# Modulation vectors of a two-layer diffusion step: two k tiles per TensorE visit in layer 0, and layer 1's second-norm shift and scale on VectorE during layer 0's FFN

## The chip, the cores and the metric

One NeuronCore of a Trainium2 chip runs the whole program. The metric is device time in microseconds (us), of which less is better. TensorE (PE) multiplies matrices, VectorE (DVE) and ScalarE (ACT) work elementwise, GpSimd (POOL) helps, and SyncE (SP) issues nearly all loads. Each of these runs its own stream of instructions in the order in which the program wrote it.

## The reference, cut to what matters

Two layers work on 384 tokens of 1,024 channels (128 context tokens and 256 latent tokens). Each layer computes six modulation vectors from a conditioning vector, for the context (`c_ctx`) and for the latents (`c`):

```
mod = (silu(cvec) @ w_mod + b_mod)                 # cvec: 1024, w_mod: 1024 x 6144, per layer
sh1, sc1, g1, sh2, sc2, g2 = split(mod, 6)         # v = 0, 1, 2, 3, 4, 5 in the kernel
hn = rmsnorm(x, g_norm1) * (1 + sc1) + sh1
x = x + g1 * mixer(hn)                             # attention, gated linear attention, pooling, gates, w_out
hn = rmsnorm(x, g_norm2) * (1 + sc2) + sh2
x = x + g2 * ((silu(hn @ w_ff_gate) * (hn @ w_ff_up)) @ w_ff_down)
```

The change concerns only when, and on which engine, those vectors of `w_mod` are computed. One vector takes eight k tiles of `w_mod`, each 128 x 1024 numbers (512 KB).

## The kernel before, in words

**Weights.** A class `Kern` first plans a list of segments (`seg`) and then plays it (`run`, with `pump` between segments). Every big weight tile is a *unit*: SP loads it into one of `RAWB` = 4 buffers `raw` (512 KB, or 448 KB for a 7-tile piece of `w_ff_down`; line 1170 issues most of them), ACT copies it into a rounded high part `wh` (line 151), DVE subtracts to get the low part `wl` (line 155), and `mm3` (line 219) multiplies: `wh` by both parts of the activations and `wl` by the high part, so 24 matmuls of 384 columns for eight k tiles, 21 for seven. There are `HB` = 3 pairs of `wh` and `wl`, so the split runs two units ahead of PE. A `raw` buffer is free again when its `wl` is done. `pump` issues the load of a unit only when the unit four places earlier in the ring has been freed, and the buffer that a load gets is the one that the program released longest ago.

**Modulation tiles** use the same ring of `raw` buffers, but are not split. They come in two kinds:

- `mod_vec` (lines 462 to 477): four TensorE matmuls per k tile (line 472) take the tile straight from `raw`; the buffer is free when PE has read it. `filler` (line 516) puts one such k tile into the plan at each call: after each `rb` tile and after each gate tile of the mixer's branches, 24 places per layer. Layer 0 uses them for vectors 2, 4 and 3 (24 tiles), layer 1 for vectors 4 and 3 (16 tiles). One such k tile is called a *visit* below.
- `mod_vec_acc` (line 483): per k tile two DVE instructions add to the two sums `P` and `A` (line 496 for the first k tile, line 498 for the other seven). The buffer is free when the second has run. After the eighth tile `fin` waits five turns and then lets PE add over the partitions by eight `pick` matmuls (line 510, four on `P` and four on `A`, each with two records in the trace); `mod_fin` (line 520) copies the result (line 523), waits and transposes it (line 530). The next vector's `P` and `A` use the same memory, so its line 496 must wait for those picks.

`accq` is the queue of DVE tiles of an FFN; `acc_step` puts the next of them into the plan. Layer 0's FFN has 32 of them: vector 5 of layer 0 and vectors 1, 0 and 2 of layer 1. Layer 1's FFN has 8.

**FFN** (`plan_ffn`): 22 pairs of a gate and an up unit; after each pair j > 1 one `acc_step`. Then the down projection: 8 output tiles n, each of three pieces of 8, 7 and 7 k tiles, 24 pieces in all; after every second piece one `acc_step`, as long as there is something in `accq`:

```
if (n * 3 + k0 // 7) % 2:
    self.acc_step()
```

So in layer 0 there are 20 steps behind gate/up pairs and 12 in the down projection. After it the row stage loads the first 256 KB tiles of layer 1's mixer (line 1183).

Of the kernel before, what the change touches and what calls it, by code (L numbers as in the profile page):

```python
# [15 lines left out]
KT = D // 128  # L16
# [14 lines left out]
class Kern:  # L31
    def __init__(self, ctx, tc, a, o):
        self.tc, self.nc, self.a, self.o = tc, tc.nc, a, o
        pool = lambda n, b, **k: ctx.enter_context(tc.tile_pool(name=n, bufs=b, **k))
        self.sb = pool("sb", 1)
        self.ps = pool("ps", 1, space=bass.MemoryType.PSUM)
        self.units = []
        self.segs = []
        self.threads = []
        self.wt = {}  # L40
        self.raw = {}
        self.n_split = 0
        self.n_raw = 0
        self.n_held = 0
        self.freed = set()
        self.ringpos = []
        self.n_ring = 0
        self.split_lim = 0
        self.mid_used = {}
        self.fillq = []  # L50
        self.accq = []
        self.htmp = {}
        self.pool_sub = set()
        self.low = []
        self.pend = set()
        self.late = []
        self.mark = 0
        self.modT = {}
        self.modfin = {}
        self.vec = {}  # L60
        self.nctr = 0
        self.sa_i = 0
        self.held = []
# [420 lines left out]
    def mod_vec_acc(self, l, v):  # L484

        st = {}

        def step(kt):
            def fn(u):
                nc = self.nc  # L490
                if kt == 0:
                    st["acc"] = [self.t(n, [128, 1024]) for n in ("P", "A")]
                for c, acc in enumerate(st["acc"]):
                    s = self.sc[:, kt, c:c + 1]
                    if kt == 0:
                        nc.vector.tensor_scalar(acc, self.raw[u], s, None, op0=ALU.mult)
                    else:
                        nc.vector.scalar_tensor_tensor(out=acc, in0=self.raw[u], scalar=s, in1=acc,  # L498
                                                       op0=ALU.mult, op1=ALU.add)
                if kt == KT - 1:  # L500
                    self.modfin[l, v] = self.spawn(fin())
            return [self.mod_unit(l, v, kt)], fn, 0

        def fin():
            for _ in range(5):
                yield
            ps = self.psa()
            for c, acc in enumerate(st["acc"]):
                for j in range(4):
                    self.nc.tensor.matmul(ps[32 * j:32 * j + 32, 0:256], self.pick[:, 32 * c:32 * c + 32],  # L510
                                          acc[:, j * 256:j * 256 + 256], start=c == 0, stop=c == 1,
                                          tile_position=(0, 32 * j))
            yield from self.mod_fin(l, v, ps)
        return [lambda kt=kt: step(kt) for kt in range(KT)]

    def filler(self):
        if self.fillq:
            self.seg(*self.fillq.pop(0)(None))

    def mod_fin(self, l, v, ps):  # L520
        nc = self.nc
# [979 lines left out]
    def plan_ffn(self, l, final):  # L1501
# [3 lines left out]
        def act_g(pg):  # L1505
            tt = self.t("tt", [128, T], bufs=2)
            nc.scalar.activation(tt, pg, AF.Tanh, scale=0.5)  # L1507
            self.late.append(lambda: nc.vector.scalar_tensor_tensor(
                out=tt, in0=tt, scalar=1.0, in1=pg, op0=ALU.add, op1=ALU.mult))
            return tt  # L1510
# [13 lines left out]
        def first(u, i):  # L1524

            ps = st[i] = self.pd() if i else self.psa(hold=True)

            def after(k):
                if i == 0 and k == 4:
                    st["norm"] = self.norm()  # L1530
                    next(st["norm"])
                if i == 1 and k == 2:
                    st["rs"] = next(st["norm"])
                    self.run_low()
                if i == 1:
                    self.hn_after(k, 3, l, 32, 24, st.get("rs"), (4, 1))
                if i == 1 and k == 3:
                    st["bb"] = self.t("rsmall", [128, 2, 2])
                    st["rest"] = self.post(st["t"][0], st[0], st["rs"], st["bb"][:, 0])
                    self.held.clear()  # L1540
            if i == 1:
                st["t"] = self.t("kn", [128, T]), self.t("KA", [128, T])
            self.mm_side((ps[:, 0:T + 2],), (u,), self.xw, after, 0)
# [23 lines left out]
        for j in range(NF):  # L1567
            ug, uu = ucol("w_ff_gate", j), ucol("w_ff_up", j)
            if j == 0:
                self.seg([ug], lambda u: first(u, 0))  # L1570
                self.seg([uu], lambda u: first(u, 1))
            elif j == 1:
                self.seg([ug, uu], second)
            else:
                hold = {}

                def fg(u, hold=hold):
                    ps = self.pd()
                    self.mm3(ps[:, 0:T], u, KT, self.xs, 0, True, True)
                    hold[0] = act_g(ps[:, 0:T])  # L1580

                def fu(u, j=j, hold=hold):
                    ps = self.pd()
                    self.mm3(ps[:, 0:T], u, KT, self.xs, 0, True, True)
                    act_u(j, hold[0], ps[:, 0:T])
                self.seg([ug], fg)
                self.seg([uu], fu)
            if j > 1:
                self.acc_step()

        us = tuple((lambda k, z=z: st["u"][k // 4][z][:, k % 4, :]) for z in range(2))
        for n in range(KT):
            hold = {}
            if not final and n == 6:
                self.seg([], lambda: self.load_gl(l + 1), 0)
            for k0, nk in ((0, 8), (8, 7), (15, 7)):
                u = self.unit((l, "fd", n, k0), self.w_cols(a["w_ff_down"][l], n * 128, nk=nk, k0=k0), nk * 128)

                def fn(u, n=n, k0=k0, nk=nk, hold=hold):
                    if k0 == 0:  # L1600
                        self.flush()
                        hold[0] = self.pd()
                    ps = hold[0][:, 0:T]
                    self.mm3(ps, u, nk, us, k0, k0 == 0, k0 == 15)
                    if k0 == 15:
                        if n == 0:
                            self.join(self.modfin[l, 5])
                        self.residual(l, n, ps, 40)
                        if final:
                            g_ = self.spawn(self.out_tile(n))  # L1610
                            if n == KT - 1:
                                self.join(g_)
                        else:
                            self.ssq_add(n)
                            st.setdefault("pre", []).append(n)
                            if n == 5:
                                self.load_sqrt()
                    if not final and n >= 4 and st["pre"]:
                        if not st.get("joined"):
                            st["joined"] = True  # L1620
                            for v in range(2):
                                self.join(self.modfin[l + 1, v])
                        self.pre(l + 1, st["pre"].pop(0), 8, 0)
                self.seg([u], fn)
                if (n * 3 + k0 // 7) % 2:
                    self.acc_step()

    def acc_step(self):
# [19 lines left out]
@with_exitstack  # L1648
def tile_hybrid_dit_step(ctx: ExitStack, tc: tile.TileContext, a, o):
    k = Kern(ctx, tc, a, o)  # L1650
    k.RAWB, k.HB = 4, 3
    with tc.manual_schedule():
        for l in range(L):
            for v in (2, 4, 3) if l == 0 else (4, 3):
                k.fillq += k.mod_vec(l, v)
        for l in range(L):
            k.plan_layer(l)
            for ll, v in ((l, 5), (l + 1, 1), (l + 1, 0), (l + 1, 2)):
                if ll < L:
                    k.accq += k.mod_vec_acc(ll, v)  # L1660
            k.plan_ffn(l, l + 1 == L)
            assert not k.accq
        assert not k.fillq
        k.head()
        k.run()
# [66 lines left out]
```

## Time and profile before

| what | value |
|---|---|
| median of 3 runs | 1341.04 us (1338.82 to 1345.76) |
| the profiled execution's own time | 1340.77 us |
| its span on the core | 1338.6 us |
| mean granted clock of TensorE | 0.989 |
| DVE, ACT, POOL busy | 859.0 us (64%), 597.3 us (45%), 194.6 us (15%) |
| DMA queue of SP | 196.68 MB, 52.1% of 16 engines |

The span is the time between the first and the last instruction on the core; the run's own time has 2.2 us around it. A busy share is the time in which an engine works on instructions. For a wait, the trace gives the idle time and what ended it, in the form `[4.14 <-DMA raw]`.

### The profile page before, as it was taken

The page shows a single profiled execution, that of the slowest core. Times are in us where ns is not written, and L with a number is a line of the kernel's source. Part 1 is how long each engine was busy: PE and PEld are TensorE (multiplying, and loading weights), DVE is VectorE, ACT ScalarE, POOL GpSimd, SP SyncE. Part 2 cuts the span into 40 slices and gives each one's busy share as a digit, 9 for nine tenths or more (in the row PEclk, how much of TensorE's full clock was granted, in tenths as well). Part 3 has the DMA queues.
Part 4 walks back from the last instruction along what each step waited for, and adds up shares of the span by engine and source line. Part 5 has one row for each costly group of instructions (what it writes and reads, how often), then busy time and mean ns, then how long its engine had stood idle before and what let it go on. Part 6 is the DMA issues. An engine that isn't in the chain of part 4 may idle for free.

```text
span 1338.6 us, 23459 instructions
## 1 busy us (share of the span) xinstructions
PE 1297.1 (97%) x9285; PEld 1205.5 (90%) x9285; DVE 859.0 (64%) x1500; ACT 597.3 (45%) x1104; POOL 194.6 (15%) x232
## 2 busy tenths in 40 slices
PE   6998999999999999999999899999999999999998
PEld 4786788889998999999988777888999899999998
DVE  4497866354568768676877987754546777544432
ACT  5655365343356333332446644543435643333221
POOL 1177000010033000000123850001101300000000
PEclk9998999999999999999999999999999999999999
DMA  9942454656543656665745325456344366444442
GB/s 288 242 102 80 144 143 131 166 146 180 151 126 110 193 172 201 177 197 170 206 135 144 102 83 165 121 154 174 95 126 126 95 185 192 143 126 120 127 133 61
DMA packets 297788, 198.51 MB, mean 148 GB/s; under 512 B 24560, under 2 KB 282384, under 8 KB 297680
## 3 DMA queue, kind: packets, MB, share of 16 engines
q1 hardware_dynamic: 296928, 196.68, 52.1%
q8 instruction: 73, 1.20, 0.4%
q0 software_dynamic: 608, 0.28, 0.1%
q14 instruction: 35, 0.29, 0.1%
q10 hardware_dynamic: 144, 0.07, 0.0%
HBM read 194.64 MB, written 2.36 MB: 147 GB/s over the span
## 4 chain that ended last, share of the span: by engine, by line
PE 81%; DVE 7%; DMA 3%; issue 3%; ACT 3%; POOL 1%; SPq 1%; ACTq 0%; DVEq 0%; POOLq 0%
PE d L219 59%; PE d L1418 8%; PE d L1350 2%; DMA m<-in_w_mod_dram 2%; PE m L472 2%; DVE wl L155 1%; DMA raw<-in_w_in_dram 1%; PE s L1109 1%; PE s L1064 1%; DVE m L797 1%; PE s L1098 1%; PE s L942 1%; DVE m L799 1%; DVE m L787 1%; DVE m L789 1%
## 5 line engine op out<-in xcount | busy, mean ns | idle before, releaser
L155 DVE TENSOR_TENSOR wl<-raw,wh 128x1024 fp32r<-128x1024 f32 (+2 forms) x274 | 330.0, 1207 | 128.4 <-ACT wh L151 122.8
L151 ACT ACTIVATE wh<-raw 128x1024 fp32r<-128x1024 f32 (+2 forms) x276 | 280.0, 1017 | 178.2 <-PE d L219 61.5
L219 PE MATMUL d<-hl,wh 128*128 128x384 f32 x1248 | 253.1, 341 | 0.0
L219 PE MATMUL d<-hh,wh 128*128 128x384 f32 x1248 | 250.0, 343 | 2.0 <-DVE vf L624 2.0
L219 PE MATMUL d<-hh,wl 128*128 128x384 f32 x1248 | 243.8, 338 | 0.0
L219 PEld LDWEIGHTS d<-hh,wh 128*128 128x128 f32 x1248 | 217.3, 189 | 17.1 <-issue 11.0
L219 PEld LDWEIGHTS d<-hl,wh 128*128 128x128 f32 x1248 | 219.0, 189 | 2.0 <-issue 0.3
L219 PEld LDWEIGHTS d<-hh,wl 128*128 128x128 f32 x1248 | 220.7, 190 | 0.0
L219 PE MATMUL d<-m,wh 128*128 128x384 f32 x896 | 165.9, 337 | 0.0
L219 PEld LDWEIGHTS d<-m,wh 128*128 128x128 f32 x896 | 155.7, 188 | 0.4 <-issue 0.4
L251 ACT ACTIVATE m<-tt 128x384 fp32r<-128x384 f32 x60 | 31.3, 525 | 155.7 <-DVE tt L1520 124.3
L219 PE MATMUL d<-m,wl 128*128 128x384 f32 x448 | 87.4, 336 | 0.0
L219 PEld LDWEIGHTS d<-m,wl 128*128 128x128 f32 x448 | 78.6, 188 | 0.0
L1418 PE MATMUL d<-m,wh 128*128 128x384 f32 x384 | 72.2, 341 | 0.0
L1418 PEld LDWEIGHTS d<-m,wh 128*128 128x128 f32 x384 | 66.0, 188 | 6.6 <-issue 5.8
L1438 POOL TENSOR_TENSOR m<-m,tt 128x384 f32<-128x384 f32 x16 | 17.0, 1083 | 340.6 <-DVE tt L1436 340.6
L561 POOL TENSOR_TENSOR ssq<-ssq,ev 128x384 f32<-128x384 f32 x18 | 29.5, 1637 | 250.6 <-ACT ev L559 250.5
L710 DVE SCALAR_TENSOR_TENSOR x<-d,modT,x 128x128 f32<-128x128 f32 x64 | 23.6, 412 | 54.7 <-PE d L219 46.9
L1401 ACT ACTIVATE tt<-d 128x384 f32<-128x384 f32 x48 | 23.6, 492 | 70.4 <-PE d L219 63.6
L1520 DVE TENSOR_TENSOR tt<-tt,d 128x384 f32<-128x384 f32 x42 | 23.2, 553 | 47.7 <-PE d L219 47.6
L1507 ACT ACTIVATE tt<-d 128x384 f32<-128x384 f32 x42 | 20.6, 489 | 63.5 <-PE d L219 59.6
L498 DVE SCALAR_TENSOR_TENSOR A<-raw,sc,A 128x1024 f32<-128x1024 f32 x35 | 47.0, 1343 | 0.0
(319 smaller groups left out, 1640.8 us busy)
## 6 DMA issues: line engine op xcount, KB each, us to landing
raw<-in_w_mod_dram SPq DMA_DIRECT2D x80, 512.0 KB, 3.8
raw<-in_w_in_dram SPq DMA_DIRECT2D x76, 512.0 KB, 4.0
raw<-in_w_ff_gate_dram SPq DMA_DIRECT2D x44, 512.0 KB, 4.9
raw<-in_w_ff_up_dram SPq DMA_DIRECT2D x44, 512.0 KB, 4.5
raw<-in_w_ff_down_dram SPq DMA_DIRECT2D x32, 448.0 KB, 4.4
m<-in_w_mod_dram SPq DMA_DIRECT2D x16, 512.0 KB, 7.3
raw<-in_w_in_dram SPq DMA_DIRECT2D x32, 256.0 KB, 3.8
raw<-in_w_out_dram SPq DMA_DIRECT2D x16, 512.0 KB, 4.1
```

Of the source, the lines that this page charges most:

```text
L151: nc.scalar.activation(h[:, f], w[:, f], AF.Copy)
L155: e.tensor_tensor(l[:, f], w[:, f], h[:, f].bitcast(F32), op=ALU.subtract)
L219: nc.tensor.matmul(ps, w[:, k * width + col:k * width + col + 128], xs[xi](k0 + k), start=first and n == 0, stop=last and n == tot - 1)
L251: self.nc.scalar.activation(h, v, AF.Copy)
L472: nc.tensor.matmul(st["ps"][32 * j:32 * j + 32], self.sc[:, kt, :], self.raw[u][:, j * 256:j * 256 + 256], start=kt == 0, stop=kt == KT - ...
L498: nc.vector.scalar_tensor_tensor(out=acc, in0=self.raw[u], scalar=s, in1=acc, op0=ALU.mult, op1=ALU.add)
L561: e.tensor_tensor(self.ssq, self.ssq, sq, op=ALU.add)
L710: nc.vector.scalar_tensor_tensor(out=self.x[n][:, c0:c1], in0=ps[:, c0:c1], scalar=self.modT[l][:, fg + n, v:v + 1], in1=self.x[n][:, c0:c ...
L1350: nc.tensor.matmul(vps[c], (self.hl if z else self.hh)[kk][:, c * 128:c * 128 + 128], w[:, k * 512:k * 512 + 512], start=kk == 0 and w is ...
L1401: nc.scalar.activation(tt, ps[:, 0:T], AF.Tanh, scale=0.5)
L1418: nc.tensor.matmul(ps[i], w[:, k * 256 + i * 128:k * 256 + i * 128 + 128], x2[xi](k), start=w is h and xi == 0 and k == 0, stop=w is lo an ...
L1520: nc.vector.tensor_tensor(tt, tt, pu, op=ALU.mult)
```

## The change

Five edits:

1. `fin` waits one turn instead of five before the picks.
2. `filler` acts at every second call only, and then puts two k tiles into the plan, one right behind the other. It takes them from the same 24 places of layer 0.
3. The list of layer 1's `filler` is empty: the 16 visits of layer 1 are gone.
4. Vectors 4 and 3 of layer 1 join `accq` of layer 0's FFN: 48 DVE steps instead of 32. In gate/up a second `acc_step` follows a pair with even j, unless the number of tiles left in `accq` is a multiple of eight. That gives eight double steps (j = 2, 4, 6, 8, 10, 14, 16, 20) and 28 steps in gate/up.
5. The other 20 steps are in the down projection: one after every piece but those with index 0, 8 and 16 (and after index 23 none is left). The same line serves layer 1's FFN, whose eight steps are already used up in gate/up.

```diff
         def fin():
-            for _ in range(5):
-                yield
+            yield
             ps = self.psa()
...
     def filler(self):
-        if self.fillq:
-            self.seg(*self.fillq.pop(0)(None))
+
+        self.n_fill += 1
+        if self.n_fill % 2 == 0:
+            for f in self.fillq[:2]:
+                self.seg(*f(None))
+            del self.fillq[:2]
...
             if j > 1:
                 self.acc_step()
+                if not final and j % 2 == 0 and len(self.accq) % KT:
+                    self.acc_step()
...
-                if (n * 3 + k0 // 7) % 2:
+                if (n * 3 + k0 // 7) % 8:
                     self.acc_step()
...
-            for v in (2, 4, 3) if l == 0 else (4, 3):
+            for v in (2, 4, 3) if l == 0 else ():
                 k.fillq += k.mod_vec(l, v)
...
-            for ll, v in ((l, 5), (l + 1, 1), (l + 1, 0), (l + 1, 2)):
+            for ll, v in ((l, 5), (l + 1, 1), (l + 1, 0), (l + 1, 2), (l + 1, 4), (l + 1, 3)):
```

Three places show how the instructions move. Line numbers of the changed kernel are one higher near line 480 (482 for 481, 499 for 498, 156 for 155) and four higher from line 520 on (1174 for 1170, 714 for 710).

SP's loads in the middle of layer 0's down projection, before; `raw_...` is a buffer, `in_w_mod` a modulation tile, `in_w_ff_down` a weight piece:

```order
L481 DMA raw_6215<-in_w_mod_dram 128x1024
L1170 DMA raw_6271<-in_w_ff_down_dram 128x7x128
L1170 DMA raw_6276<-in_w_ff_down_dram 128x8x128
L481 DMA raw_6278<-in_w_mod_dram 128x1024
L1170 DMA raw_6333<-in_w_ff_down_dram 128x7x128
L1170 DMA raw_6338<-in_w_ff_down_dram 128x7x128
```

and now:

```order
L482 DMA raw_6191<-in_w_mod_dram 128x1024
L1174 DMA raw_6193<-in_w_ff_down_dram 128x7x128
L482 DMA raw_6226<-in_w_mod_dram 128x1024
L1174 DMA raw_6228<-in_w_ff_down_dram 128x7x128
L482 DMA raw_6261<-in_w_mod_dram 128x1024
L1174 DMA raw_6263<-in_w_ff_down_dram 128x8x128
L482 DMA raw_6292<-in_w_mod_dram 128x1024
L1174 DMA raw_6294<-in_w_ff_down_dram 128x7x128
```

Two weight pieces stood between two modulation tiles, and now one does.

DVE at the same place, before (line 155 makes `wl` of a piece, line 498 adds a modulation tile, line 710 adds an output tile to the residual):

```order
L498 SCALAR_TENSOR_TENSOR P_5842<-raw_6149,sc_122,P_5842 128x1024
L498 SCALAR_TENSOR_TENSOR A_5843<-raw_6149,sc_122,A_5843 128x1024
L155 TENSOR_TENSOR wl_6274<-raw_6271,wh_6273 128x896
L155 TENSOR_TENSOR wl_6307<-raw_6276,wh_6306 128x1024
L498 SCALAR_TENSOR_TENSOR P_5842<-raw_6215,sc_122,P_5842 128x1024
L498 SCALAR_TENSOR_TENSOR A_5843<-raw_6215,sc_122,A_5843 128x1024
```

and now:

```order
L499 SCALAR_TENSOR_TENSOR P_5971<-raw_6133,sc_122,P_5971 128x1024
L499 SCALAR_TENSOR_TENSOR A_5972<-raw_6133,sc_122,A_5972 128x1024
L156 TENSOR_TENSOR wl_6231<-raw_6228,wh_6230 128x896
L499 SCALAR_TENSOR_TENSOR P_5971<-raw_6191,sc_122,P_5971 128x1024
L499 SCALAR_TENSOR_TENSOR A_5972<-raw_6191,sc_122,A_5972 128x1024
L156 TENSOR_TENSOR wl_6266<-raw_6263,wh_6265 128x1024
L499 SCALAR_TENSOR_TENSOR P_5971<-raw_6226,sc_122,P_5971 128x1024
L499 SCALAR_TENSOR_TENSOR A_5972<-raw_6226,sc_122,A_5972 128x1024
```

A modulation tile is now added between every two splits; when `raw_6228` is split, the tiles `raw_6191`, `raw_6226` and `raw_6261` of the list above wait for their turn.

PE at the first `rb` tiles of layer 0's mixer, before (line 472 is a visit, line 219 a weight unit, line 1064 attention scores):

```order
L472 MATMUL m_1827<-raw_1431,sc_122 32x256 x4
L219 MATMUL d_1839<-hh_72,wh_1677 128x384 x8
L219 MATMUL d_1839<-hl_73,wh_1677 128x384 x8
L219 MATMUL d_1839<-hh_72,wl_1678 128x384 x8
L1064 MATMUL s_286_1870<-KA_1700,m_138_650 128x384
L1064 MATMUL s_288_1876<-KA_1700,m_138_650 128x384
L472 MATMUL m_1827<-raw_1588,sc_122 32x256 x4
```

and now:

```order
L220 MATMUL d_1832<-hh_72,wh_1677 128x384 x8
L220 MATMUL d_1832<-hl_73,wh_1677 128x384 x8
L220 MATMUL d_1832<-hh_72,wl_1678 128x384 x8
L1068 MATMUL s_284_1863<-KA_1700,m_138_650 128x384
L1068 MATMUL s_286_1869<-KA_1700,m_138_650 128x384
L473 MATMUL m_1875<-raw_1480,sc_122 32x256 x4
L473 MATMUL m_1875<-raw_1588,sc_122 32x256 x4
```

Two visits stand side by side where one stood after each tile; in layer 1's mixer there is no row of line 473 at all.

## Rows read from the trace of the kernel before

**Rows 1.** Page, busy time of the engines, and the chain's share by engine
```profile
PE 1297.1 (97%) x9285; PEld 1205.5 (90%) x9285; DVE 859.0 (64%) x1500; ACT 597.3 (45%) x1104; POOL 194.6 (15%) x232
...
PE 81%; DVE 7%; DMA 3%; issue 3%; ACT 3%; POOL 1%; SPq 1%; ACTq 0%; DVEq 0%; POOLq 0%
```
**Rows 2.** Timeline of DVE, a modulation step in gate/up and what follows it
```profile
437.53 1.28 DVE L498 SCALAR_TENSOR_TENSOR P<-raw,sc,P 128x1024 f32<-128x1024 f32 x1
...
439.92 0.55 DVE L252 TENSOR_TENSOR m<-tt,m 128x384 fp32r<-128x384 f32 x1
```
**Rows 3.** Timeline of PE, a visit in layer 0 (start us, us, then the work)
```profile
307.33 0.64 PE L472 MATMUL m<-raw,sc 128*32 128x256 f32 x8
307.90 3.04 PE L1418 MATMUL d<-m,wh 128*128 128x384 f32 x16
```
**Rows 4.** Timeline of PE, a visit in layer 1
```profile
820.35 0.91 PE L1064 MATMUL s<-KA,m 64*128 64x384 f32 x2 [2.17 <-ACT pr L1080]
821.19 0.74 PE L472 MATMUL m<-raw,sc 128*32 128x256 f32 x8
821.86 2.61 PE L219 MATMUL d<-hh,wh 128*128 128x384 f32 x7
```
**Rows 5.** Windows of line 472 alone: us, PE busy (x), PEld busy (x), clock, DMA
```profile
796.00:839.00 43.00, 3.93 (x48) 0.95 (x48) 0.96 0.52 151
839.00:945.00 106.00, 6.39 (x80) 1.57 (x80) 1.00 0.53 145
```
**Rows 6.** Timeline of PE, the two halves of a pick set
```profile
631.72 0.64 PE L510 MATMUL s<-P,pick 128*32 128x256 f32 x8
632.17 0.61 PE L510 MATMUL s<-A,pick 128*32 128x256 f32 x8
632.72 1.49 PE L219 MATMUL d<-m,wh 128*128 128x384 f32 x7
```
**Rows 7.** Windows, all engines: us, PE, PEld, DVE, ACT, POOL busy; clock, DMA, GB/s
```profile
437.06:445.38 8.32, 8.32 (x50) 8.32 (x49) 6.33 (x8) 3.03 (x4) 0.00 (x0) 1.00 0.75 215
589.48:682.49 93.01, 93.01 (x548) 92.14 (x547) 67.43 (x79) 33.65 (x56) 9.98 (x14) 1.00 0.64 186
```
**Rows 8.** Timeline of SP, loads at layer 0's `rb` tiles
```profile
158.13 0.38 SPq L1170 DMA_DIRECT2D raw<-in_w_in_dram  x1
164.49 0.38 SPq L1390 DMA_DIRECT2D raw<-in_w_br_c_dram  x1
```
**Rows 9.** Timeline of ACT, the copy of that unit
```profile
162.15 1.06 ACT L151 ACTIVATE wh<-raw 128x1024 fp32r<-128x1024 f32 x1 [3.25 <-DMA raw<-in_w_in_dram]
```
**Rows 10.** Timeline of DVE, the splits of the unit before it and of that unit
```profile
156.88 1.23 DVE L155 TENSOR_TENSOR wl<-raw,wh 128x1024 fp32r<-128x1024 f32 x1 [1.59 <-ACT wh L151]
...
163.24 1.23 DVE L155 TENSOR_TENSOR wl<-raw,wh 128x1024 fp32r<-128x1024 f32 x1 [1.11 <-ACT wh L151]
```
**Rows 11.** Timeline of SP, weight pieces in layer 0's down projection
```profile
617.49 1.50 SPq L1170 DMA_DIRECT2D raw<-in_w_ff_down_dram  x2
...
624.65 3.69 SPq L1170 DMA_DIRECT2D raw<-in_w_ff_down_dram  x2
```
**Rows 12.** Timeline of ACT, the copy of the first of them
```profile
622.54 0.95 ACT L151 ACTIVATE wh<-raw 128x896 fp32r<-128x896 f32 x1 [5.98 <-DMA raw<-in_w_ff_down_dram]
```
**Rows 13.** Timeline of DVE, its split
```profile
623.53 1.09 DVE L155 TENSOR_TENSOR wl<-raw,wh 128x896 fp32r<-128x896 f32 x1 [2.54 <-ACT wh L151]
```
**Rows 14.** DMA issues of 590 to 680 us: count, KB, median us to landing
```profile
raw<-in_w_ff_down_dram SPq DMA_DIRECT2D x14, 448.0 KB, 4.5
raw<-in_w_mod_dram SPq DMA_DIRECT2D x11, 512.0 KB, 3.9
...
raw<-in_w_in_dram SPq DMA_DIRECT2D x4, 256.0 KB, 2.6
```
**Rows 15.** The same of 1165 to 1250 us, the end of layer 1
```profile
raw<-in_w_ff_down_dram SPq DMA_DIRECT2D x6, 448.0 KB, 3.7
raw<-in_w_ff_down_dram SPq DMA_DIRECT2D x3, 512.0 KB, 4.1
```

More of the change, by code (lines that the diff above doesn't have):

```diff
@@ L47, in __init__ @@
         self.n_ring = 0
+        self.n_fill = 0
         self.split_lim = 0
```

## Prediction

> **What bounds the kernel now.** First the page's busy shares and the shares of the chain of waits: PE is busy for 97% of the span and holds 81% of the chain; no other engine is above 64% or 7% [rows 1]. So a part of PE's work that goes away is time gained where PE has no gaps, and work given to DVE is free only while PE still gets its split weights in time. I then asked stage by stage, with windows. In gate/up a pair takes 8.32 us, PE is busy for all of it and DVE for 6.33; in layer 0's down projection PE is busy for all 93.01 us, which is 93.01 / 24 = 3.88 us a piece, and DVE for 67.43 [rows 7]. DVE seems to have room in both. The question is what else the change takes up: the four `raw` buffers.
>
> **Layer 1's mixer: 16 visits go.** A visit moves what follows it on PE by 307.90 - 307.33 = 0.57 us in layer 0 [rows 3] and by 821.86 - 821.19 = 0.67 in layer 1 [rows 4]; six of the 16 lie between 796 and 839 us and ten between 839 and 945 (48 and 80 records of eight a visit), and PE spends 3.93 + 6.39 = 10.3 us on them, drains included [rows 5]. I take 16 x 0.62 = 9.9. Their buffers also stop taking turns with the weights: PE waited 2.17 us for a softmax that stood on ACT behind a `wh` whose load was late [rows 4], and I count that wait as gone. Together **-12**. Bounds: -14 with 0.7 a visit and a further wait of the kind gone; -5 if half the visits lay in time that PE would lose anyway.
>
> **Layer 0's mixer: 24 visits become 12 pairs.** The nearest row to two visits in a row is a set of picks, four matmuls on `P` and four on `A` of the same shape: 0.45 us for the first half and 0.55 for the second [rows 6]. So a pair costs 1.00 where two visits cost 1.14 to 1.34; 12 pairs give -1.7 to -4. Against that, two of four buffers are held at once. I take **-2**, from -5 to +4 (two more waits of 2 us like those of rows 4).
>
> **Gate/up of layer 0: eight more DVE steps.** A step is two instructions and moves what follows it on DVE by 439.92 - 437.53 = 2.4 us [rows 2]. A pair with a double step needs 6.33 + 2.4 = 8.7 us of DVE against 8.32, but the next pair has a single step: 15.1 against 16.64 [rows 7]. That fits on average. `fin` now gives PE the picks one turn after the last step instead of five. Where the sum is not yet finished, PE would wait itself: with a double step behind j = 6 the second sum ends about 5.2 us after the pair's first turn and the picks come after 4.2, and a late split could add to that. Earlier picks also free `P` and `A` sooner for the next vector, which can only help DVE. I take **+1**, from 0 to +3.
>
> **The down projection of layer 0: 12 steps become 20.** By busy time it would fit: 67.43 + 8 x 2.4 = 86.6 us of DVE in 93 [rows 7]. But a buffer with a modulation tile is held until DVE has added the tile, and tiles are loaded early. By the order shown above, when a piece is split, three modulation tiles are parked in three of the four buffers. One buffer is left for weights, so a piece can't be loaded until the piece before it has been split. That is a loop: load, `wh`, `wl`, next load. It runs once in the trace of before at each place where loads alternate one to one: at layer 0's `rb` tiles SP issues a weight load at 158.13, just when the `wl` of 156.88 (1.23 us) is done; ACT starts its copy at 162.15 having waited for the load, DVE its `wl` at 163.24, and SP the next load at 164.49 [rows 8 to 10]. One turn is 6.36 us there. The units of that stage are slow enough to hide most of it; a down piece takes 3.88.
>
> For a down piece the turn is the landing and what follows. Behind the landing, `wh` to `wl` to the next issue is 624.65 - 622.54 = 2.11 us for 448 KB [rows 11 to 13] and 164.49 - 162.15 = 2.34 for 512 KB [rows 8, 9]. Landings: 4.5 us for 448 KB in this stage now [rows 14], 3.7 and 4.1 in the quieter end of layer 1 [rows 15], and 622.54 - 617.49 = 5.05 in the piece shown [rows 11, 12]. With one weight and about one modulation tile (960 KB) in 6 us the stage moves less than the 186 GB/s of now [rows 7], so I take values nearer the quiet ones, 3.9 and 4.1. The turn is then (2 x (3.9 + 2.11) + 4.1 + 2.34) / 3 = 6.15, and each piece loses 6.15 - 3.88 = 2.27 us. Twenty pieces have a step behind them: 20 x 2.27 = 45.4. From that go the two pieces that are split ahead when the loop begins, 2 x 3.88 = 7.8, and about one turn's loss at each of the two places without a step, where two weights can be in flight, 2 x 2.3 = 4.6. That leaves **+33**. The two more sets of picks that now fall here (1.0 us each) and the waits of line 496 lie inside PE's gaps.
>
> Bounds: with the quiet landings of rows 15 the turn is (2 x 5.81 + 6.44) / 3 = 6.0 and the loss +31; with 5.05 for all it is 7.24, and 20 x 3.36 - 7.8 - 6.7 = +53. What can make it smaller is a landing below any seen for this size; the 2.6 us that 256 KB takes [rows 14] is the lower end, 1.3 us below the 3.9 of 512 KB there. Halfway, 3.1, gives a turn of 5.3 and 20 x 1.42 - 7.8 - 2.8 = +18.
>
> The Trainium skill has a price for that landing ("DMA: Bandwidth & Descriptors", section "Anatomy of one DMA — SWDGE (gpsimd) path"): about 2.0 us fixed plus the bytes over 436 GB/s, fitted for DMAs issued by GpSimd. For 448 KB that is 3.05 us and for 512 KB 3.20, an estimate by that page; the down projection would then lose about +19 and the whole would be 1347. The rows of this kernel, issued by SP and sharing the queue, are 0.6 us and more above it in every group [rows 14, 15], so it serves as the lesser case here.
>
> **Layer 1's FFN.** It keeps its eight steps; only its picks come earlier. Zero, with DVE's slack in gate/up as cover [rows 7].
>
> **Sum.** -12 - 2 + 1 + 33 = +20 against the profiled execution's own 1340.77 us: 1360.8. That execution is 0.3 us from the median of the three runs, so the forecast is **1361 us**.
>
> **Rivals.**
> - *The buffers keep up* (ends faster). If the order in which buffers come free lets a weight's load start one piece earlier than I read it, two loads are in flight and a turn carries two pieces: 6.15 / 2 = 3.1 us, below 3.88. PE then stays full, and only two sets of picks are added in the FFN. The point of decision is 3.88 us a piece. For it: DVE has 86.6 us of work in 93. Against: the SP order, and the row at 158.13, which starts with the `wl` of the unit directly before. Time: 1340.8 - 12 - 2 + 1 + 2 = 1330.
> - *The loop is there but short*: landings near 3.1 us because only two transfers share the queue. Time: 1340.8 - 14 + 1 + 18 = 1346.
> - *The loop is longer*: DMAs of a modulation tile and a weight get in each other's way as in the 5.05 us piece. Time: 1340.8 - 14 + 3 + 53 = 1383.
> - *The change doesn't give what it removes*: layer 1's mixer keeps waits on ACT and the windows get shorter by 5 us and not 12; with +4 in layer 0 that gives 1340.8 - 5 + 4 + 1 + 33 = 1374.
>
> **How the numbers follow.** Forecast 0.55 (1350 to 1368), rival one 0.10, rival two 0.14, rival three 0.13, rival four 0.08. Faster and slower count from 0.5%, about what a measurement of this kernel can tell from no change: 1334 and 1348. Rival one ends faster, with a little for gains that I don't see: 0.11. Rival two lies on the edge, about half of it within 0.5%, and a mixture of rivals adds some: 0.09. The rest is slower: 0.80. The range leaves out rival one, the lower part of rival two and the far end of rival three: 1345 to 1384.
>
> **What would show it.** Right: in layer 0's down projection PE's busy share falls from 100% to some 65 to 75%, the stage takes about 126 us and not 93, pieces start some 6 us apart, ACT's `wh` waits for `in_w_ff_down` most of the time between them, and SP's weight load is released by the `wl` of the piece before. Layer 1's mixer ends about 12 us sooner after its start. Wrong: the stage still takes 93 to 97 us with PE full (rival one), or landings of 3 us (rival two). If gate/up grows by over 3 us, the double steps cost what I put at nothing.

## The result and the profile after

The changed kernel takes 1374.84 us (median of 4 runs, 1371.95 to 1376.96) where the kernel before takes 1340.47 in the same comparison: a ratio of 1.025, with a 95% interval of 1.022 to 1.027. It is slower, by more than the 1361 us that I forecast and within the range of 1345 to 1384.

The page of the changed kernel, busy time and the chain's shares, answers to [rows 1]:

```profile
PE 1296.5 (94%) x9189; PEld 1207.7 (88%) x9189; DVE 894.5 (65%) x1532; ACT 597.7 (44%) x1104; POOL 194.4 (14%) x232
...
PE 64%; DVE 13%; DMA 11%; ACT 5%; issue 4%; POOL 1%; SPq 1%; ACTq 0%; DVEq 0%; POOLq 0%
```

PE is busy for as long as before, with 96 matmul records fewer. What grew is the span, and the chain now runs over DMA for 11% of it where it was 3%: the program waits for loads. Where, the windows say. First those of the kernel before that were not shown yet (gate/up of layer 0, and layer 1's mixer from its first `vb` matmul to the first activation of its FFN; columns as in [rows 7]):

```profile
419.65:589.48 169.83, 169.83 (x999) 167.75 (x999) 125.16 (x152) 65.31 (x90) 3.49 (x7) 1.00 0.64 185
...
766.54:1073.70 307.16, 299.56 (x2117) 269.24 (x2110) 194.81 (x426) 149.49 (x320) 48.15 (x46) 0.99 0.44 125
```

Then the same stages of the changed kernel, with the down projection between them, which answers to the second of [rows 7]:

```profile
419.58:604.37 184.79, 174.05 (x1018) 168.92 (x1017) 141.03 (x169) 65.67 (x91) 3.47 (x7) 0.99 0.64 191
604.37:732.37 128.00, 104.53 (x582) 96.37 (x581) 88.78 (x103) 34.57 (x57) 12.54 (x14) 0.93 0.57 170
817.10:1109.00 291.90, 286.29 (x1984) 264.70 (x1978) 194.22 (x423) 148.86 (x317) 48.74 (x46) 0.99 0.37 102
```

So gate/up took 15.0 us more, the down projection 35.0 more, and layer 1's mixer 15.3 less. The beginning up to layer 0's FFN (419.65 and 419.58), the row stage (84.0 and 84.7) and layer 1's FFN (264.9 and 265.0) hardly differ. The sum, -0.1 + 15.0 + 35.0 + 0.7 - 15.3 + 0.1 = 35.4, is the whole difference of the spans (1374.0 - 1338.6).

The loop that I forecast stands in the timeline of the changed kernel's down projection (SP, ACT, DVE and PE together):

```profile
655.77 1.09 DVE L156 TENSOR_TENSOR wl<-raw,wh 128x896 fp32r<-128x896 f32 x1 [2.03 <-ACT wh L152]
...
656.90 0.37 SPq L1174 DMA_DIRECT2D raw<-in_w_ff_down_dram  x1
...
660.64 1.06 ACT L152 ACTIVATE wh<-raw 128x1024 fp32r<-128x1024 f32 x1 [4.90 <-DMA raw<-in_w_ff_down_dram]
...
661.73 1.23 DVE L156 TENSOR_TENSOR wl<-raw,wh 128x1024 fp32r<-128x1024 f32 x1 [2.47 <-ACT wh L152]
...
661.75 3.05 PE L220 MATMUL d<-m,wh 128*128 128x384 f32 x16 [0.81 <-ACT wh L152]
...
662.99 0.37 SPq L1174 DMA_DIRECT2D raw<-in_w_ff_down_dram  x1
...
666.86 0.95 ACT L152 ACTIVATE wh<-raw 128x896 fp32r<-128x896 f32 x1 [5.16 <-DMA raw<-in_w_ff_down_dram]
...
667.85 1.09 DVE L156 TENSOR_TENSOR wl<-raw,wh 128x896 fp32r<-128x896 f32 x1 [2.49 <-ACT wh L152]
...
667.87 2.70 PE L220 MATMUL d<-m,wh 128*128 128x384 f32 x14 [1.68 <-ACT wh L152]
...
668.97 0.37 SPq L1174 DMA_DIRECT2D raw<-in_w_ff_down_dram  x1
```

Each weight load is issued when the `wl` of the piece before is done (655.77 + 1.09 = 656.86, then 656.90), ACT waits about 5 us for it, and PE starts with the `wh`. The turns are 662.99 - 656.90 = 6.09 us and 668.97 - 662.99 = 5.98; the forecast had 6.15. The landings, from the issue to the start of ACT's copy, are 3.74 us for 512 KB and 3.87 for 448 KB; over the whole stage the trace's medians are 4.1 and 3.8, and the forecast had 4.1 and 3.9. The Trainium skill ("DMA: Bandwidth & Descriptors", section "Anatomy of one DMA — SWDGE (gpsimd) path") has a fit for DMAs that GpSimd issues, by which these loads would take 3.20 and 3.05 us, an estimate by that page. The two landings shown, issued by SP, lie 0.5 and 0.8 us above it; they don't agree with it.

What I had not forecast is the same loss in gate/up. The timeline where the first double step stands:

```profile
435.71 2.44 SPq L482 DMA_DIRECT2D raw<-in_w_mod_dram  x2
...
440.67 1.22 DVE L156 TENSOR_TENSOR wl<-raw,wh 128x1024 fp32r<-128x1024 f32 x1 [1.96 <-ACT wh L152]
...
441.92 0.38 SPq L1174 DMA_DIRECT2D raw<-in_w_ff_gate_dram  x1
...
445.90 1.06 ACT L152 ACTIVATE wh<-raw 128x1024 fp32r<-128x1024 f32 x1 [2.98 <-DMA raw<-in_w_ff_gate_dram]
...
447.01 1.66 PE L220 MATMUL d<-hh,wh 128*128 128x384 f32 x8 [1.73 <-ACT wh L152]
...
474.52 0.64 PE L510 MATMUL s<-P,pick 128*32 128x256 f32 x8 [3.62 <-DVE P L499]
```

Two modulation tiles are asked for together; the next gate tile can be loaded only at 441.92, when the `wl` of 440.67 frees a buffer, and PE waits 1.73 us. Before the picks it waits 3.62 us more for the sum. Over the whole stage PE waits 4.0 us for `wh` and 6.7 before picks, where the kernel before has no wait.

### The profile page after: what moved, and what is told of

Same layout as the page of the kernel before. It is cut to its first block, busy times and chain, and to the rows that moved or that the text cites. A ratio compares the mean times of both kernels' runs of the same rounds, so it can differ in the third digit from the quotient of the medians.

```text
span 1374.0 us, 23312 instructions
## 1 busy us (share of the span) xinstructions
PE 1296.5 (94%) x9189; PEld 1207.7 (88%) x9189; DVE 894.5 (65%) x1532; ACT 597.7 (44%) x1104; POOL 194.4 (14%) x232
## 4 chain that ended last, share of the span: by engine, by line
PE 64%; DVE 13%; DMA 11%; ACT 5%; issue 4%; POOL 1%; SPq 1%; ACTq 0%; DVEq 0%; POOLq 0%
PE d L220 44%; PE d L1422 7%; DMA raw<-in_w_ff_down_dram 5%; DMA raw<-in_w_ff_up_dram 3%; DVE wl L156 3%; ACT wh L152 3%; PE d L1354 2%; DMA m<-in_w_mod_dram 2%; DVE A L499 1%; DVE P L499 1%; PE s L1113 1%; PE s L1068 1%; DVE m L801 1%; DVE ev L660 1%; PE s L1102 1%
## 5 line engine op out<-in xcount | busy, mean ns | idle before, releaser
L220 PE MATMUL d<-m,wh 128*128 128x384 f32 x896 | 170.7, 344 | 10.8 <-ACT wh L152 10.8
L220 PEld LDWEIGHTS d<-m,wh 128*128 128x128 f32 x896 | 158.6, 192 | 15.0 <-ACT wh L152 13.4
L1422 PE MATMUL d<-m,wh 128*128 128x384 f32 x384 | 72.0, 341 | 0.0
L1422 PEld LDWEIGHTS d<-m,wh 128*128 128x128 f32 x384 | 66.1, 188 | 5.5 <-issue 3.7
L499 DVE SCALAR_TENSOR_TENSOR A<-raw,sc,A 128x1024 f32<-128x1024 f32 x49 | 65.0, 1326 | 0.0
L499 DVE SCALAR_TENSOR_TENSOR P<-raw,sc,P 128x1024 f32<-128x1024 f32 x49 | 62.7, 1279 | 0.0
L1405 ACT ACTIVATE tt<-d 128x384 f32<-128x384 f32 x48 | 23.6, 491 | 59.0 <-PE d L220 50.6
```

The costliest lines, as they stand in the source:

```text
L220: nc.tensor.matmul(ps, w[:, k * width + col:k * width + col + 128], xs[xi](k0 + k), start=first and n == 0, stop=last and n == tot - 1)
L1405: nc.scalar.activation(tt, ps[:, 0:T], AF.Tanh, scale=0.5)
L1422: nc.tensor.matmul(ps[i], w[:, k * 256 + i * 128:k * 256 + i * 128 + 128], x2[xi](k), start=w is h and xi == 0 and k == 0, stop=w is lo an ...
```

## The experiments

The theory, **buffers**: modulation tiles that wait for DVE hold the `raw` buffers, so weights are loaded one at a time, in the down projection and at the double steps. Its rivals: **DVE work** (the added steps themselves delay the splits) and **early picks** (one turn is too short, and PE waits for unfinished sums). Stage times in us, each from the profile of its run: gate/up and down are layer 0's, rows is the row stage behind them, mixer is layer 1's.

| run | gate/up | down | rows | mixer | time, us |
|---|---|---|---|---|---|
| before | 169.8 | 93.0 | 84.0 | 307.2 | 1340.5 |
| the change | 184.8 | 128.0 | 84.7 | 291.9 | 1374.8 |
| shift | 168.4 | 122.8 | 84.3 | 304.1 | 1368.1 |
| small | 181.4 | 125.8 | 83.6 | 292.2 | 1371.1 |
| fin5 | 181.7 | 132.0 | 90.7 | 292.2 | 1383.6 |
| half | 169.8 | 126.7 | 83.9 | 304.2 | 1373.6 |
| novis | 169.8 | 93.0 | 84.1 | 295.0 | 1330.2 |
| pairs | 169.8 | 93.0 | 84.0 | 307.9 | 1343.1 |
| m11 | 172.2 | 136.2 | 83.6 | 292.0 | 1371.9 |
| m11b | 172.6 | 115.2 | 85.1 | 291.9 | 1353.8 |
| m11b_fin5 | 171.2 | 114.8 | 91.4 | 292.4 | 1356.0 |
| best5 | 232.8 | 97.4 | 86.1 | 292.0 | 1394.7 |
| best1 | 234.7 | 93.2 | 87.9 | 292.1 | 1396.9 |
| two_tiles | 172.5 | 94.9 | 84.4 | 292.1 | 1332.6 |

### shift: the same work, only moved (kernel before)

```diff
-            if j > 1:
+            if j > (1 if final else 6):
                 self.acc_step()
...
-                if (n * 3 + k0 // 7) % 2:
+                if (n * 3 + k0 // 7) % (2 if final else 8):
                     self.acc_step()
```

> The kernel before, with its 32 DVE steps only moved: none behind the pairs j = 2 to 6 of layer 0's gate/up, and in the down projection one after every piece but every eighth, so 17 steps there and not 12. Nothing is added or removed. Theory 'buffers' (one weight in flight where modulation tiles alternate with pieces): gate/up stays at 170 us, the down projection goes from 93 to 108 to 122, the whole 1355 to 1370. Theory 'DVE work': 5 more steps of 2.4 us fit into the free 25 us, so down stays under 96 and the whole under 1344.

Measured: 1368.05 us in one run. Five DVE steps moved into the down projection made that stage 29.8 us longer; some 2 us of this are two sets of picks that moved there with them. Its window, and three rows of SP and PE in it:

```profile
589.83:712.66 122.83, 105.88 (x582) 100.48 (x582) 80.52 (x93) 34.73 (x58) 12.40 (x14) 0.92 0.56 165
```
```profile
644.94 0.37 SPq L1170 DMA_DIRECT2D raw<-in_w_ff_down_dram  x1
...
650.03 4.62 PE L219 MATMUL d<-m,wh 128*128 128x384 f32 x16 [2.27 <-ACT wh L151]
...
651.26 0.37 SPq L1170 DMA_DIRECT2D raw<-in_w_ff_down_dram  x1
```

DVE is busy for 80.5 us of 122.8, and the loads are 6.3 us apart. This is the loss of the down projection without any of the change's other parts. DVE work as the cause falls: 5 steps are 12 us, and there was room for them. Traffic as the cause falls too: the queue moved 165 GB/s in this stage and 170 in the changed kernel's, less than the 186 of the kernel before [rows 7] and the 220 of `two_tiles` below, each with PE full.

### small: the tiles without the work (changed kernel)

```diff
-                        nc.vector.scalar_tensor_tensor(out=acc, in0=self.raw[u], scalar=s, in1=acc,
+                        nc.vector.scalar_tensor_tensor(out=acc[:, 0:w], in0=self.raw[u][:, 0:w], scalar=s, in1=acc[:, 0:w],
```

with `w` = 8 in layer 0's FFN, from the second k tile of each vector on.

> The changed kernel, which in layer 0's FFN adds only 8 of the 1024 columns of each modulation tile on DVE (the rest of the sums is left out); loads, buffers and order stay. Theory 'buffers': tiles stay parked until DVE comes to them, the down projection is still 108 to 126 us, the whole 1345 to 1365. Theory 'DVE work': the down projection is 93 to 97 us and gate/up 170, the whole 1320 to 1328. Theory 'early picks': the sums are finished in time, so the waits before the picks go and the whole is 1345 to 1355, with no waits for wh in the down projection left.

Measured: 1371.08 us in one run, 3.8 below the changed kernel. The window of the down projection and two steps in it:

```profile
602.16:727.94 125.78, 104.04 (x582) 96.93 (x581) 47.25 (x103) 34.40 (x58) 10.18 (x14) 0.95 0.56 175
```
```profile
653.22 0.37 SPq L1175 DMA_DIRECT2D raw<-in_w_ff_down_dram  x1
...
657.55 1.06 ACT L152 ACTIVATE wh<-raw 128x1024 fp32r<-128x1024 f32 x1 [5.63 <-DMA raw<-in_w_ff_down_dram]
...
659.78 0.22 DVE L500 SCALAR_TENSOR_TENSOR P<-raw,sc,P 128x8 f32<-128x8 f32 x1
...
659.89 0.37 SPq L1175 DMA_DIRECT2D raw<-in_w_ff_down_dram  x1
```

An addition now takes 0.22 us, DVE's busy time in the stage fell from 88.8 to 47.3 us, and the stage from 128.0 to 125.8. The loads still come 659.89 - 653.22 = 6.67 us apart. The 1371 lies above what "buffers" gave for this run (1345 to 1365); that range leaves room for 126 us of down projection only if gate/up falls too, and it stayed at 181.4. The split of causes is plain all the same: with nearly half of DVE's work in the stage gone, most of the loss stays.

### fin5: five turns before the picks (changed kernel)

```diff
-            yield
+            for _ in range(5):
+                yield
             ps = self.psa()
```

> The changed kernel, with five turns between the last DVE step of a vector and its picks, as before the change. Theory 'buffers': the waits of PE before the picks (some 18 us in layer 0's FFN) are time in which the weights catch up, so little of it comes back: 1362 to 1373. Theory 'early picks': all of it comes back and the slower clock behind those waits too: 1345 to 1355. Theory 'DVE work': within 4 us of 1375.

Measured: 1383.64 us (1382.08 to 1387.60), ratio to before 1.032 (1.029 to 1.034): slower than the changed kernel, which no theory gave. PE's waits in the down projection (us in total, times, longest):

```profile
PE d L220 <- ACT wh L152: 27.3, 18, 2.5
```

In the changed kernel there were 10.8 us of waits for `wh` and 12.5 before picks. Now no wait stands before picks and 27.3 us before `wh`. The wait had only changed its place; while PE stood before the picks, weights were loaded and split. Early picks are not the cause. Gate/up became 3.1 us shorter by the later picks, the down projection 4.0 longer and the row stage 6.0 longer.

### half: one vector fewer, no double steps (changed kernel)

```diff
+            for v in (2, 4, 3) if l == 0 else (3,):
...
+            for ll, v in ((l, 5), (l + 1, 1), (l + 1, 0), (l + 1, 2), (l + 1, 4)):
```

and the second `acc_step` in gate/up is taken out.

> The changed kernel, with no double steps in gate/up; layer 1's vector 3 stays on TensorE, as four pairs of visits in its mixer, so that only vector 4 moves (40 DVE steps: 20 in gate/up, 20 in down). Theory: the 15 us that gate/up lost come from the double steps, so gate/up is 170 to 173 us; the down projection stays near 128; layer 1's mixer loses half of what it gained (some 7 us). The whole 1362 to 1371. Rival: gate/up lost its time to the early picks, which stay here, so it is 178 or more.

Measured: 1373.63 us in one run, 2.6 above what I expected. Gate/up is 169.8 us with the early picks still in it, so its loss comes with the double steps. The down projection keeps its loss. Layer 1's mixer gained only 3.0 us: its four pairs of visits brought a wait of 4.0 us for a softmax, which was not there with single visits.

### pairs and novis: the two edits to the visits alone (kernel before)

`pairs` has the changed `filler` and nothing else, and `novis` leaves 12 of layer 1's 16 visits out:

```diff
-        return [lambda mid, kt=kt: step(kt, mid) for kt in range(KT)]
+        return [lambda mid, kt=kt: step(kt, mid) if l == 0 or kt in (0, KT - 1) else None for kt in range(KT)]
```

> The kernel before, with the paired visits alone, in both layers. The changed kernel's trace shows layer 0's mixer ending at the same time as before (419.6 us), so I expect 0 for layer 0 and within 2 us of it for layer 1: 1338 to 1343. A theory by which a pair saves part of a visit's drain: 1333 to 1337.

> The kernel before, with 12 of layer 1's 16 visits left out (each of its two vectors gets the first and the last k tile only). Theory: PE sets the pace of layer 1's mixer, so it gets 12 x 0.62 = 7.4 us shorter and 2 us more where a softmax waited behind a late load: 1330 to 1334. Rival: the visits lie in time that PE loses anyway: 1337 to 1341.

Measured: `pairs` 1343.05 us and `novis` 1330.18, one run each. `pairs` moves nothing that can be told from no change. PE's waits up to layer 0's FFN show why, first before, then in the changed kernel:

```profile
PE s L1064 <- ACT pr L1080: 2.0, 1, 2.0
```
```profile
PE s L1113 <- ACT pr L1084: 3.0, 1, 3.0
...
PE s L1102 <- ACT tt L1374: 0.9, 1, 0.9
...
PE s L1068 <- ACT pr L1084: 0.6, 1, 0.6
```

2.0 us of waits for ACT became 4.5: the visits' own time on PE fell from 15.3 to 12.9 us, and these waits take that back. In `novis` the mixer is 12.1 us shorter for 12 visits, more than 7.4 and 2. Of the 2.2 us wait of [rows 4] nothing is left, and neither is what stood behind it. In the kernel before, PE's granted clock was 0.50 there, the lower of its two levels (columns as in [rows 7]):

```profile
821.60:825.00 3.40, 3.40 (x16) 3.15 (x11) 2.93 (x10) 1.11 (x2) 0.00 (x0) 0.50 0.82 238
```

Seven matmuls took 2.61 us in it [rows 4], where eight take 1.55 at 421.03. At half the clock the stretch cost about 1.7 us, so a visit was worth (12.1 - 2.2 - 1.7) / 12 = 0.68 us. The changed kernel gives nearly the same from PE's busy time, (299.56 - 286.29 - 1.7) / 16 = 0.72. The unchanged mixer itself took 304.1 us in `shift` and 307.2 before; `shift` has 0.6 us of that wait and a clock of 1.00 behind it.

### m11 and m11b: another place for the added tiles (changed kernel)

The tile `m11` is idle in the FFN and takes the place of a fifth buffer:

```diff
                 if not final and j % 2 == 0 and len(self.accq) % KT:
-                    self.acc_step()
+                    self.acc_step(11)
...
-                    self.acc_step()
+                    self.acc_step(None if (n * 3 + k0 // 7) % 2 else 11)
...
-            return [self.mod_unit(l, v, kt)], fn, 0
+            return [self.mod_unit(l, v, kt, mid)], fn, 0
```

`acc_step` and `step` of `mod_vec_acc` hand the argument on; `mod_unit` with it loads into that tile and not into `raw`.

> The changed kernel, with the added modulation tiles of layer 0's FFN (the second one of a double step, and every second one in the down projection) loaded into the tile m11, which is idle in the FFN, and not into the four raw buffers. DVE does the same work, PE the same picks, the same bytes are loaded. Theory 'buffers' (modulation tiles parked in raw starve the weights): gate/up of layer 0 falls from 184.8 us to 170 to 175, the down projection from 128.0 to 93 to 105, the whole from 1375 to 1325 to 1345. Theory 'DVE work' (24 us and more of added steps delay the splits on DVE): within 5 us of 1375. Theory 'early picks' (PE waits for sums that are not finished): within 8 us of 1375, with waits of 4 to 5 us before the picks still there.

Measured: 1371.92 us (1371.20 to 1373.62). Gate/up fell to 172.2 us, as "buffers" said, with the same DVE work, the same picks and the same bytes. But the down projection rose to 136.2, and by its total the run answers to the two rivals (within 5 and within 8 us of 1375) and not to "buffers". The timeline of the down projection shows why:

```profile
639.91 0.37 SPq L1174 DMA_DIRECT2D raw<-in_w_ff_down_dram  x1
...
648.71 1.28 DVE L499 SCALAR_TENSOR_TENSOR A<-m,sc,A 128x1024 f32<-128x1024 f32 x1
...
650.02 0.34 SPq L482 DMA_DIRECT2D m<-in_w_mod_dram  x1
650.45 0.39 SPq L1174 DMA_DIRECT2D raw<-in_w_ff_down_dram  x1
```

For 10 us, from 639.91 to 650.02, SP issued no load. It stood at the next tile for `m11` until DVE had added the last one (648.71 + 1.28 = 649.99), and the weight load at 650.45 stood behind it. A new wait had taken the old one's place. In `m11b` the load for `m11` comes one piece later in SP's order:

```diff
+                i = n * 3 + k0 // 7
+                if self.accq and i % 8 and i % 2 == 0:
+                    piece(*pieces[i + 1])
```

> As the run m11, but in the down projection the load of a tile for m11 stands behind the next weight piece in SP's order, and not ahead of it. In the run m11 gate/up fell to 172 us, but the down projection took 136: SP stood at the load of the next m11 tile until DVE had added the last one, and that came behind the split of a piece not yet loaded. Theory 'buffers, and SP's order': down 95 to 110 us, the whole 1335 to 1350. Rival 'dense steps cost the same in any buffer' (traffic, or DVE's order): down 120 us or more, the whole 1355 or more.

Measured: 1353.77 us (1353.22 to 1354.71), ratio 1.009 (1.007 to 1.012). One place in SP's order was worth 21 us of the down projection. At 115.2 us the stage still lies 5 us above the band of "buffers" and 5 below that of its rival, and the whole lies between the two bands as well.

### m11b_fin5: are the picks the rest?

> The run m11b with five turns between the last DVE step and the picks. In m11b the down projection of layer 0 still takes 115 us, with 9 us of PE waiting before picks and 5 us for wh. Theory: with a buffer more the weights are no longer behind, so the early picks are now what PE waits for: down 98 to 106 us, the whole 1338 to 1345. Rival: as in the run fin5, the waits for picks only turn into waits for wh: down 113 to 120 us, the whole 1352 to 1360.

Measured: 1356.02 us in one run. The rival holds: down is 114.8 us, and 12.1 us of waits for `wh` stand where the waits for picks were. SP's longest wait in that stage is again for an added tile (us in total, times, longest):

```profile
SPq L482 <- DVE A L499: 49.9, 8, 8.9
```

So the rest of `m11b` is again a matter of loads that stand behind one another.

### best5 and best1: fewer tiles in the down projection

In both, 33 steps stand in gate/up and 15 in the down projection:

```diff
-                if not final and j % 2 == 0 and len(self.accq) % KT:
+                if not final and j % 5 != 1 and len(self.accq) % KT:
                     self.acc_step(11)
...
-                if (n * 3 + k0 // 7) % 8:
+                if i % 2 or i in (4, 12, 20):
```

> The run m11b with five turns before the picks and the 48 steps put elsewhere: 33 behind gate/up pairs (13 double steps, the second one always in m11) and 15 in the down projection, 12 of them after every second piece as before the change and three in m11. Theory 'buffers': raw holds modulation tiles as thinly as before the change, so gate/up is 171 to 174 us and the down projection 94 to 99, layer 1's mixer keeps its 15 us, and the whole is 1328 to 1335, faster than both kernels. Rival: DVE has 126.6 + 13 x 2.4 = 158 us of work in gate/up's 170 and its splits come late now and then: gate/up 176 or more, the whole 1338 to 1345.

> The run best5 with one turn before the picks, as in the changed kernel. Theory: PE waits 1 to 5 us at some of the six sets of picks: 4 to 12 us more than best5. Rival: one turn is as good as five: within 2 us of best5.

Measured: `best5` 1394.69 us (1392.64 to 1397.20), `best1` 1396.87 (1394.23 to 1398.68). Both `best5` ranges were missed, "buffers" (1328 to 1335) and its rival (1338 to 1345): gate/up took 232.8 us. The theory was right on the down projection, which is back at 97.4 and 93.2 us. Five turns or one before the picks made a difference of 2.2 us, which the spread of the runs can't tell from none. SP's waits in gate/up of `best5`, and its timeline at one double step:

```profile
SPq L482 <- DVE A L499: 109.7, 17, 12.0
```
```profile
498.33 1.28 DVE L499 SCALAR_TENSOR_TENSOR A<-m,sc,A 128x1024 f32<-128x1024 f32 x1
...
499.64 0.34 SPq L482 DMA_DIRECT2D m<-in_w_mod_dram  x1
500.07 0.39 SPq L1175 DMA_DIRECT2D raw<-in_w_ff_gate_dram  x1
```

Where two pairs in a row use `m11`, SP stands at its load until the tile before it has been added, and the next gate tile stands behind. It is the wait of `m11` in another stage.

### two_tiles: a tile for each of two pairs in a row

```diff
-                    self.acc_step(11)
+                    self.acc_step(11 - j % 2)
...
-                if i % 2 or i in (4, 12, 20):
+                if i % 2 or i in (4, 10, 14, 20):
```

> All 48 steps on DVE in layer 0's FFN, 33 of them in gate/up (13 double steps; the second tile in m11 behind even pairs and in m10 behind odd ones, so that each of the two is asked for again after two pairs at the earliest) and 15 in the down projection (11 behind odd pieces, and m11 behind pieces 4, 10, 14 and 20, loaded one piece later), with two turns before the picks. In the run best5 one tile m11 for pair after pair made SP wait up to 12 us for DVE with the next gate load behind it. Theory 'buffers, and SP's order': with two tiles nothing waits, gate/up 171 to 175 us, down 93 to 98, layer 1's mixer keeps its 15 us: 1328 to 1336, faster than both kernels. Rival: 13 double steps are too much for DVE, or SP still waits for a modulation tile: gate/up 185 us or more, the whole 1342 or more.

Measured: 1332.55 us (1331.05 to 1335.12, 6 runs); ratio to before 0.993, with an interval of 0.991 to 0.995. It is 3% faster than the changed kernel and 0.7% faster than the kernel before (1341.32 in the same comparison), a small gain, but one that the interval tells from none. Its windows of gate/up and the down projection:

```profile
423.43:595.91 172.48, 172.48 (x1034) 168.70 (x1034) 152.01 (x179) 66.81 (x92) 3.49 (x7) 1.00 0.74 220
595.91:690.77 94.86, 94.64 (x566) 92.58 (x566) 75.71 (x90) 33.86 (x57) 14.46 (x14) 1.00 0.66 198
```

PE is full again in both, with all 48 steps on DVE, which is busy for 152.0 of 172.5 us in gate/up. The two stages cost 4.5 us more than before, and layer 1's mixer keeps 15.1 us of gain. The idea of the change was sound; what cost the time was where the tiles waited and what waited behind them.

## Why the prediction was right or wrong

Forecast +20, measured +34 by the medians and +35.4 by the spans.

| term | forecast (bounds) | measured by the spans |
|---|---|---|
| layer 1's mixer | -12 (-14 to -5) | -15.3 |
| layer 0's mixer | -2 (-5 to +4) | -0.1 |
| layer 0's gate/up | +1 (0 to +3) | +15.0 |
| layer 0's down projection | +33 (+18 to +53) | +35.0 |
| row stage | - | +0.7 |
| layer 1's FFN | 0 | +0.1 |

**The down projection was right, in mechanism and in size.** One weight in flight, turns of 6 us, loads released by the `wl` before: all stand in the rows of the changed kernel, and `shift` shows that they need nothing but the order of the tiles. The way of the sum was not quite what happened. I had 20 turns that each lose 2.3 us of PE's time. In the trace PE waits for `wh` only seven times (10.8 us); it also waits 12.5 us at the picks, which the sum put inside PE's gaps and in which the loads catch up; the other 11.5 us are more busy time, part of it at the lower clock (below). So PE's busy share is 82% and not the 65 to 75% that I named as a sign. The loads keep the loop's pace even so: the five turns from the load at 607.86 to the one at 638.59 take 6.15 us each, and the five from 650.44 to 681.82 take 6.28. `fin5`, where the picks don't wait, has 18 waits for `wh`, 27.3 us, and a stage of 132.0: the loop as I had reckoned it.

**The step that failed is gate/up**: "That fits on average", and the +1. I weighed the double steps by DVE's time alone (15.1 us against 16.64) and by the picks, with about 1 us for a late sum where PE waited 6.7. The prediction named the sign for it, a growth of over 3 us, and it came. `small` shows that DVE's time mattered little there (181.4 us with almost no adding). `half` and `m11` show what did: with no double steps, or with their second tile out of `raw`, the stage is at 169.8 and 172.2 us. It was the rule that I used one paragraph later for the down projection, that a parked modulation tile takes a buffer from the weights, and I didn't apply it to two tiles asked for at once.

**Layer 1's mixer** was mis-sized, within its mechanism. The wait for the softmax went as forecast (2.0 us less of idle time); a visit is worth about 0.7 us and not 0.62; and the 1.7 us at the lower clock behind that wait had no term in the sum. **Layer 0's mixer** gained nothing, since the pairs' waits grew by 2.5 us.

Of the rivals, "the buffers keep up" is excluded by the turns of 6 us, and the short loop by the landings. "The loop is longer" (1383) is excluded by them too: the landings were as forecast. "The change doesn't give what it removes" gave 1374, almost exactly the measured time, and that is luck: its -5 and +4 for the mixers were -15.3 and -0.1, and the 15.0 us of gate/up are not in it.

Two sentences of the prediction on the Trainium skill's fit ("DMA: Bandwidth & Descriptors", section "Anatomy of one DMA — SWDGE (gpsimd) path") need correcting. Worked out as the other cases, 3.05 and 3.20 us give a loss of +17.5 and not +19. And not every group of [rows 14, 15] lies 0.6 us above the fit: for 256 KB it gives 2.60 us, an estimate by that page, and [rows 14] have 2.6.

## What to carry to other kernels

When work is moved from a full engine to one with idle time, ask what its operands occupy while they wait: a shared ring of buffers can be full while the engine that empties it is busy for 69% of the stage (88.78 of 128.00 us), and then the loads of the critical work run one at a time. Look at the order of the loads and count how many tiles are parked at each point; two requests in a row count double. And a buffer of its own helps only if its load doesn't stand at the head of the in-order load queue waiting for it to come free: put that load later in the order, or alternate between two buffers.

## What the runs showed of the hardware that I had not expected

PE's clock fell behind its long waits. In the changed kernel PE stood idle for 5.56 us before the picks at 683.04; windows of that wait and of the 6 us after it (columns as in [rows 7]), and PE's rows:

```profile
677.32:683.04 5.72, 0.17 (x1) 0.00 (x0) 2.84 (x4) 1.84 (x4) 0.45 (x1) 0.76 0.47 149
683.04:689.00 5.96, 5.84 (x33) 4.16 (x34) 4.26 (x8) 1.56 (x3) 0.00 (x0) 0.66 0.59 161
```
```profile
683.04 1.08 PE L510 MATMUL s<-P,pick 128*32 128x256 f32 x8 [5.56 <-DVE P L499]
684.24 1.08 PE L510 MATMUL s<-A,pick 128*32 128x256 f32 x8
685.25 3.88 PE L220 MATMUL d<-m,wh 128*128 128x384 f32 x16
```

The granted clock is 0.76 in the wait and 0.66 in the 6 us of work behind it, a mean of its two levels (1.2 and 2.4 GHz); half a pick set takes 1.08 us where it took 0.64 [rows 6], and 16 matmuls 3.88 us where they take 3.05 at 661.75. Not every wait is followed by it: behind the waits of 0.81 to 1.79 us between 661 and 674 us the granted clock stayed at 1.00.

Over the whole down projection PE is busy for 104.5 us with 93.0 before, 11.5 more. Two more sets of picks are about 2 us of that. The granted clock is 0.50, the lower level, in these stretches, each behind or around a wait of PE of 2.4 us or more:

```profile
632.50:639.30 6.80, 5.31 (x26) 3.65 (x27) 4.34 (x7) 0.95 (x1) 0.00 (x0) 0.50 0.48 146
680.30:687.10 6.80, 3.94 (x22) 2.25 (x23) 4.83 (x6) 1.97 (x5) 0.45 (x1) 0.50 0.49 147
714.40:717.80 3.40, 3.40 (x12) 3.40 (x12) 2.28 (x2) 0.00 (x0) 0.00 (x0) 0.50 0.54 143
```

With the last 0.87 us of the stage, also at 0.50, PE is busy for 5.31 + 3.94 + 3.40 + 0.87 = 13.5 us in them; half of that, 6.8 us, is what the lower clock cost. The last 2.6 us or so no row here assigns. So a long wait of PE can cost more than its length.
